# A two-layer decoder trunk on one core: norm blocks in two tiles, sums formed at their source's split, the third block turned early, own tiles for half the output weights

## The chip, the core and the metric

The kernel runs on one core of one Trainium2 chip. The core has a matrix engine (TensorE; PE in the profile, with its weight loads as PEld), a vector engine (DVE), a scalar engine (ACT), a general engine (POOL) and an engine that issues transfers (SP). Each works off its own instructions in order; semaphores tie them together. DMA transfers are issued from SP's, ACT's and POOL's queues; the ones that add to what is already in memory go through POOL's. The metric is the device time in microseconds: 1045.73 us, the median of three runs (1043.29 to 1046.05).

## The reference

512 tokens of width 1024 pass two residual layers, each a token mixer and a gated feed-forward block, with a root-mean-square norm ahead of each and one at the end. Everything is float32.

```
def rmsnorm(x, g):
    y = xf * lax.rsqrt(jnp.mean(xf * xf, axis=-1, keepdims=True) + EPS)
    return (y * g.astype(jnp.float32)).astype(x.dtype)

def swiglu(h, w_gate, w_up, w_down):
    return jnp.einsum('bsf,fd->bsd', jax.nn.silu(g) * u, w_down)    # g, u = h @ w_gate, h @ w_up

for i in range(DEPTH):
    h = rmsnorm(x, norm_mix[i])
    y = pool_mixer(...) if i % N_MIXERS == 0 else attn_mixer(...)
    x = x + y
    h = rmsnorm(x, norm_ffn[i])
    x = x + swiglu(h, w_gate[i], w_up[i], w_down[i])
return rmsnorm(x, norm_final)
```

Layer 0 mixes by windowed means (2, 4, 8 and 16 tokens) with a projection in, a product by group and a projection out; layer 1 by dilated windowed attention with 16 heads, merged by weights over three groups of heads, and a projection out. The feed-forward width is 2816.

## The kernel before

**Products in three parts.** Every float32 operand is split into a rounded part and a rest (`hi`, `lo`): ACT casts (L137 for weights, L302 elsewhere), DVE subtracts (L138, L303). A product is three matmuls, hi x hi, hi x lo and lo x hi.

**Weights.** All weights stand in one list, `queue`, in the order in which they are used. `load` (L93) issues the transfer of an operand into a raw tile of 512 KB (`wraw`, five buffers; `vraw`, three buffers, in the feed-forward blocks alone) from SP. Where an operand is the sum of two blocks of a weight, the second block is added by a transfer on POOL's queue (L105). `weights(i)` (L118) loads up to `load_ahead` operands beyond `i` (or the operand's own `ahead`) and splits up to `split_ahead`, as long as fewer than `RING` = 5 split operands are held; split operands lie in five pairs of tiles of `wspl`.

**Feed-forward.** The products are made by a scheme of Strassen's kind: a group of columns ("quad") has seven operands, 0 to 6. Operands 0 and 3 are plain blocks, 1, 4 and 6 are loaded (1 and 4 as sums of two blocks), and 2 and 5 are formed from operand 1's raw tile by adding operand 0's, then operand 3's raw tile (`plus`, L134). Operands 1, 2 and 5 share one `vraw` tile. The add stands at the split of operand 2 or 5, so the raw tiles of operands 0 and 3 are held until then. `FFN_ORDER` says what follows what: two groups woven together (`TWO`: operands 0 and 3 of both, then 1, 2, 4, 5, 6), two to three single groups, a down projection of the groups so far (`down`, also seven operands), and so on; the last down projection is made plainly, token block by token block (L709). In the woven pair the tokens of blocks 2 and 3 arrive late, in the steps of `late`.

**Norm.** Tokens come in four blocks of 128. `Norm.add` squares half a block on ACT and sums it (L265). `inverse_rms` adds the halves (L273), takes a root on ACT (L274) and refines the inverse in four DVE steps (L275 to L282). `scale` multiplies the block with that and the gain in one DVE instruction (L290) into `xn`, of which there is one. `turn` then transposes `xn` on PE (L299), and `split` writes the tokens, feature by row, into `h` (L302, L303). `h` is written at two offsets, `tokens_at(0)` and `tokens_at(SHIFT)`, so that a new set of tokens can be written beside the old one.

**Around a mixer's end.** `out_projection` (L332) makes the left half of the columns weight by weight for all four blocks, then the right half block by block, and turns block 0 after the products of block 1 and block 1 after those of block 2. Blocks 2 and 3 are turned in the feed-forward block (L622). At the end of the first feed-forward block, blocks 0 and 1 are turned within it (L720), block 2 at the start of attention (`late(2)`, L926) and block 3 between the first products there.

**Order.** PE's instructions keep the order of the text (`manual_schedule`). Those of the other engines, transfers included, are ordered by a planner which goes by program order as priority, by `high_priority`, and by modelled times.

Of the kernel before, what the change touches and what calls it, by code (L numbers as in the profile page):

```python
# [17 lines left out]
P = 128  # L18
S = 512
# [38 lines left out]
def trunk_kernel(ctx: ExitStack, tc: tile.TileContext, x_in, xT, gam, gains, consts, ident_d, w0, wT, w1, wv, w_down, out):  # L58
# [21 lines left out]

    queue = []
# [36 lines left out]
    def weights(i, split_ahead=4, load_ahead=5, held=0):  # L118
# [7 lines left out]
        while len(ready) < min(loaded["w"], i + split_ahead) and (len(ready) <= i or len(ready) - i + held < RING):  # L126
            item = queue[len(ready)]
            if "v" not in pools and item["kind"] == "v":
                break
# [3 lines left out]
            if "plus" in item:  # L133
                nc.vector.tensor_add(raw[:, :n], raw[:, :n], raws[item["plus"]][:, :n])  # L134
            hi = wspl.tile([P, 1024], F32R, name="whi")
            lo = wspl.tile([P, 1024], F32R, name="wlo")
            nc.scalar.copy(hi[:, :n], raw[:, :n])  # L137
            nc.vector.tensor_sub(lo[:, :n], raw[:, :n], hi[:, :n].bitcast(F32))  # L138
# [8 lines left out]
    def rows_of(w):  # L147

        by = w.rearrange("(k p) c -> p k c", p=P)
        return lambda at, half: enqueue(by[:, at : at + 2, COLS[half]], (2, S), rows=True)  # L150
# [8 lines left out]
    j_out += [w_out(BY_GROUP[i], 0) for i in (2, 4, 6)] + [w_out(BY_GROUP[i], 1) for i in (0, 2, 4, 6)]  # L159

    def enqueue_ffn(layer):
# [3 lines left out]
        def operand(js, i, block, shape, ahead):  # L165
# [12 lines left out]
        def quad(n, i, ahead=8):  # L178
# [6 lines left out]
        def down(b):  # L185
# [3 lines left out]
            for i in range(7):  # L189
                for js, a, n in zip(dn[b], (at, at + 2), (2, len(pairs) - 2)):  # L190
                    operand(js, i, lambda m, k: tiles[k, :, a : a + n, COLS[m]], (n, S), 6)
# [20 lines left out]
    j_wo = [wo(2 * i, half) for half in range(2) for i in range(4)]  # L212
# [18 lines left out]
    h_both = [stat.tile([P, NC * S + SHIFT], F32R, name=f"h_{part}") for part in ("hi", "lo")]  # L231

    def tokens_at(shift):
        at = (shift, SHIFT - shift)
        return [h[:, i : i + NC * S].rearrange("p (c s) -> p c s", c=NC) for i, h in zip(at, h_both)]
# [6 lines left out]
    tmp.tile([P, 8], F32, name="gap4")  # L242
    ones = tmp.tile([P, D], F32, name="xn")[:, :P]
# [8 lines left out]
    class Norm:  # L252


        def __init__(self, i=None):
            self.ss = tmp.tile([P, 4, 2], F32, name="ss")
            if i is not None:
                self.gain = tmp.tile([P, D], F32, name="gain")
                nc.sync.dma_start(self.gain, gains[i : i + 1, :].partition_broadcast(P))
                self.xn = tmp.tile([P, D], F32, name="xn")  # L260

        def add(self, b, half):
            sq = tmp.tile([P, S], F32, name="sq")
            with tc.high_priority(URGENT):
                nc.scalar.activation(  # L265
                    sq, x[:, b, COLS[half]], AF.Square, scale=D ** -0.5, accum_out=self.ss[:, b, half : half + 1]
                )

        def inverse_rms(self, b, n=1):

            v, r0, r = (tmp.tile([P, 4], F32, name=name, bufs=2)[:, :n] for name in ("v4", "r04", "r4"))
            sums = self.ss[:, b : b + n, :]
            nc.vector.scalar_tensor_tensor(v, sums[:, :, 0], EPS, sums[:, :, 1], op0=ALU.add, op1=ALU.add)  # L273
            nc.scalar.activation(r0, v, AF.Sqrt)  # L274
            nc.vector.reciprocal(r0, r0)  # L275
            if n == 1:
                nc.vector.tensor_scalar(v, v, r0, r0, op0=ALU.mult, op1=ALU.mult)
            else:
                nc.vector.tensor_mul(v, v, r0)
                nc.vector.tensor_mul(v, v, r0)  # L280
            nc.vector.tensor_scalar(v, v, -0.5, 1.5, op0=ALU.mult, op1=ALU.add)
            nc.vector.tensor_mul(r, v, r0)  # L282
            return r

        def scale(self, b, to, parts):

            with tc.high_priority(URGENT):
# [877 lines left out]
```

## Time and profile before

| what | us |
|---|---|
| median of three runs | 1045.73 |
| the profiled execution | 1047.32 |
| its span | 1045.5 |
| PE busy in the span | 1008.1 |
| DVE busy | 796.5 |
| ACT busy | 510.4 |
| POOL busy | 122.3 |

The span is the time between the profile's first and last event; the 1.8 us between it and the execution's own time lie outside. A busy PE is not a PE at its full rate: where the granted clock falls below 1.00, matmuls start farther apart. A wait is put down to the event that came last before it ended; a row of the timeline gives start, length, engine, line, what is written from what, and in brackets the idle time before it and its releaser. The stages in the profiled execution: the pooling mixer to about 114 us, the first feed-forward block from 114 to 467, attention from 467 to 697, the second feed-forward block from 697 to the end.

### The profile page before, as it was taken

To read this page: it belongs to the slowest core of one execution; us is meant where nothing else is said; L and a number is where in the kernel's file an instruction comes from. 1 tells how busy PE (TensorE), PEld (TensorE's weight loads), DVE (VectorE), ACT (ScalarE), POOL (GpSimd) and SP (SyncE) were. 2 spreads that over 40 slices of the span, in tenths; PEclk is the share of its full clock that TensorE was granted. 3 is DMA by queue.
4 is the path that set the end of the run, shared out by engine and by line. 5 is a ranking of instruction groups with operands and counts; after the bars stand their busy time and mean duration, and the time that the engine had idled before them with its cause. 6 is when DMAs were issued, how large, how long until landed. Compare 5 with 4: busy or idle time off the path is not lost.

```text
span 1045.5 us, 16597 instructions
## 1 busy us (share of the span) xinstructions
PE 1008.1 (96%) x6582; PEld 917.3 (88%) x6582; DVE 796.5 (76%) x1122; ACT 510.4 (49%) x818; POOL 122.3 (12%) x109
## 2 busy tenths in 40 slices
PE   9999978999999999989999999999999999999997
PEld 7888878988998998979778899889898999899895
DVE  5364779897888888776988745479889798788875
ACT  5553355644553654552344443356654465365453
POOL 0000101102011100002324210100110201110000
PEclk9999989999999999999999999999999999999999
DMA  9333557668768855523211242705756965886522
GB/s 350 138 125 77 136 140 181 168 169 220 177 152 221 219 141 150 181 76 112 81 64 40 66 130 93 193 5 164 195 156 188 227 170 123 234 210 160 149 76 80
DMA packets 76349, 155.16 MB, mean 148 GB/s; under 512 B 6448, under 2 KB 6576, under 8 KB 76272
## 3 DMA queue, kind: packets, MB, share of 16 engines
q1 hardware_dynamic: 58800, 120.48, 34.9%
q0 software_dynamic: 17184, 33.36, 18.8%
q8 instruction: 51, 0.84, 0.3%
q10 hardware_dynamic: 288, 0.27, 0.1%
q14 instruction: 26, 0.21, 0.1%
HBM read 151.99 MB, written 2.10 MB: 147 GB/s over the span
## 4 chain that ended last, share of the span: by engine, by line
PE 80%; DMA 8%; DVE 7%; ACT 2%; issue 2%; POOL 0%; SPq 0%; ACTq 0%; POOLq 0%; DVEq 0%
PE p L572 21%; PE r L572 10%; PE r L658 6%; PE mm L572 5%; DMA wraw<-w 5%; PE mm L216 4%; PE mm L217 4%; PE mm L218 4%; PE p L658 3%; DMA vraw<-w 3%; PE mm L709 2%; DVE wlo L138 2%; PE mm L344 2%; PE mm L342 2%; PE mm L343 2%
## 5 line engine op out<-in xcount | busy, mean ns | idle before, releaser
L138 DVE TENSOR_TENSOR wlo<-wraw,whi 128x1024 fp32r<-128x1024 f32 (+2 forms) x198 | 227.9, 1157 | 87.8 <-ACT whi L137 87.4
L137 ACT CAST whi<-wraw 128x1024 fp32r<-128x1024 f32 (+2 forms) x198 | 192.6, 980 | 175.7 <-DMA wraw<-w 32.6
L137 ACT CAST whi<-vraw 128x1024 fp32r<-128x1024 f32 (+1 forms) x102 | 99.4, 975 | 146.1 <-DVE vraw L134 71.3
L572 PE MATMUL p<-t_hi,whi 128*128 128x256 f32 x528 | 151.9, 288 | 12.3 <-ACT keep L583 5.1
L572 PE MATMUL p<-t_hi,wlo 128*128 128x256 f32 x528 | 151.2, 286 | 1.5 <-DVE wlo L138 1.5
L572 PE MATMUL p<-t_lo,whi 128*128 128x256 f32 x528 | 150.8, 286 | 0.0
L138 DVE TENSOR_TENSOR wlo<-vraw,whi 128x1024 fp32r<-128x1024 f32 (+1 forms) x102 | 114.9, 1127 | 33.0 <-ACT whi L137 32.9
L572 PEld LDWEIGHTS p<-t_hi,whi 128*128 128x128 f32 x528 | 101.7, 193 | 14.3 <-ACT keep L583 5.9
L572 PEld LDWEIGHTS p<-t_hi,wlo 128*128 128x128 f32 x528 | 101.7, 193 | 1.9 <-DVE wlo L138 1.9
L572 PE MATMUL r<-h_hi,whi 128*128 128x256 f32 x352 | 99.9, 284 | 2.5 <-ACT h_hi L302 2.5
L572 PEld LDWEIGHTS p<-t_lo,whi 128*128 128x128 f32 x528 | 101.6, 192 | 0.0
L572 PE MATMUL r<-h_lo,whi 128*128 128x256 f32 x352 | 100.1, 284 | 1.0 <-DVE h_lo L303 1.0
L572 PE MATMUL r<-h_hi,wlo 128*128 128x256 f32 x352 | 100.1, 284 | 0.0
L134 DVE TENSOR_TENSOR vraw<-vraw,wraw 128x1024 f32<-128x1024 f32 x68 | 76.6, 1126 | 0.7
L572 PEld LDWEIGHTS r<-h_hi,whi 128*128 128x128 f32 x352 | 67.2, 191 | 2.7 <-ACT h_hi L302 2.7
L572 PEld LDWEIGHTS r<-h_lo,whi 128*128 128x128 f32 x352 | 67.0, 190 | 1.2 <-DVE h_lo L303 1.2
L572 PEld LDWEIGHTS r<-h_hi,wlo 128*128 128x128 f32 x352 | 67.1, 191 | 0.0
L216 PE MATMUL mm<-h_hi,whi 128*128 128x512 f32 (+1 forms) x176 | 66.1, 376 | 0.0
L105 POOL DMA_DIRECT2D wraw<-w x22 | 27.0, 1227 | 330.0 <-DVE x L330 106.4
L217 PE MATMUL mm<-h_lo,whi 128*128 128x512 f32 (+1 forms) x176 | 64.0, 364 | 0.0
L218 PE MATMUL mm<-h_hi,wlo 128*128 128x512 f32 (+1 forms) x176 | 63.9, 363 | 0.0
L105 POOL DMA_DIRECT2D vraw<-w x22 | 26.8, 1227 | 287.9 <-DMA vraw<-w 112.5
(289 smaller groups left out, 2518.1 us busy)
## 6 DMA issues: line engine op xcount, KB each, us to landing
wraw<-w SPq DMA_DIRECT2D x116, 512.0 KB, 4.5
wraw<-w_down SPq DMA_DIRECT2D x32, 512.0 KB, 4.1
wraw<-w POOLq DMA_DIRECT2D x22, 512.0 KB, 9.3
vraw<-w SPq DMA_DIRECT2D x22, 512.0 KB, 5.1
vraw<-w POOLq DMA_DIRECT2D x22, 512.0 KB, 7.2
wraw<-wT SPq DMA_DIRECT2D x16, 512.0 KB, 4.1
wraw<-w_down SPq DMA_DIRECT2D x24, 256.0 KB, 2.7
vraw<-w_down SPq DMA_DIRECT2D x6, 512.0 KB, 5.1
```

Of the source, the lines that this page charges most:

```text
L105: nc.gpsimd.dma_start(dst, more, accum_op=ALU.add)
L134: nc.vector.tensor_add(raw[:, :n], raw[:, :n], raws[item["plus"]][:, :n])
L137: nc.scalar.copy(hi[:, :n], raw[:, :n])
L138: nc.vector.tensor_sub(lo[:, :n], raw[:, :n], hi[:, :n].bitcast(F32))
L216: nc.tensor.matmul(ps, lhsT=whi, rhs=xhi, start=first, stop=False, **kw)
L217: nc.tensor.matmul(ps, lhsT=whi, rhs=xlo, start=False, stop=False, **kw)
L218: nc.tensor.matmul(ps, lhsT=wlo, rhs=xhi, start=False, stop=last, **kw)
L342: nc.tensor.matmul(ps, lhsT=xhi, rhs=w[0][:, k, :], start=first, stop=False)
L343: nc.tensor.matmul(ps, lhsT=xhi, rhs=w[1][:, k, :], start=False, stop=False)
L344: nc.tensor.matmul(ps, lhsT=xlo, rhs=w[0][:, k, :], start=False, stop=last)
L572: nc.tensor.matmul(ps[:, g, :], lhsT=w[:, g, c, :], rhs=xx[:, c, :], start=i in (0, 1, 3) and g + c + k == 0, stop=c == 3 and k == 2, skip ...
L658: nc.tensor.matmul(acc[t], lhsT=u, rhs=w, start=i in (0, 1, 3) and c + k == 0, stop=c == len(pairs) - 1 and k == 2, skip_group_check=True,)
```

## The change

- **Sums.** `plus` is gone. Behind the split of operand 1, operand 0's raw tile is added to operand 1's; behind the split of operand 2 or 3, whichever is later, operand 3's is. Operands 2 and 5 are then split without an add. The look-ahead of groups is 10 instead of 8, that of down projections 10 instead of 6.
- **Ring.** The four weights of the right half of each output projection get their own tiles (pool `b`, four pairs) and don't count in the ring of five; `out_projection` may split and load further ahead.
- **Norm.** A block is multiplied with the gain on DVE, half by half, as soon as it is complete (`gained`); the square's own output goes to the same tile first. Blocks 0 and 2 have one tile, 1 and 3 another (`odd_rows`). The sums are quartered and `EPS / 4` is added to the first of them. The root is taken on ACT directly from the two sums; DVE forms `1 / (v / s + s)`. ACT scales the block.
- **Third block.** `out_projection` transposes block 2 at its own end and hands the result on; the first feed-forward block turns blocks 0, 1 and 2 itself.
- **Memory.** `z` in the pooling mixer and the merged heads of attention are written over `h` at offset 0; `h` is longer by `SHIFT`, and both of its parts use the same offset. One set of window constants is loaded into a tile that the squares use. The angles get their own tile, loaded from SP instead of POOL. In the last stage the output leaves from the norm's tiles instead of `x`.

The core of the diff:

```diff
-        while len(ready) < min(loaded["w"], i + split_ahead) and (len(ready) <= i or len(ready) - i + held < RING):
+        while len(ready) < min(loaded["w"], i + split_ahead):
...
+            if "pool" not in item and len(ready) > i and held + sum("pool" not in it for it in queue[i : len(ready)]) >= RING:
                 break
...
-            if "plus" in item:
-                nc.vector.tensor_add(raw[:, :n], raw[:, :n], raws[item["plus"]][:, :n])
...
             nc.vector.tensor_sub(lo[:, :n], raw[:, :n], hi[:, :n].bitcast(F32))
+            for into, more in item.get("then", ()):
+                nc.vector.tensor_add(raws[into][:, :n], raws[into][:, :n], raws[more][:, :n])
...
-                item.update(into=js[1], plus=js[0 if i == 2 else 3])
+                item.update(into=js[1])
...
+            if i == 1:
+                item["then"] = [(js[1], js[0])]
+            elif i in (2, 3) and 2 in js and 3 in js:
+                item["then"] = [(js[1], js[3])]
...
+        def inverse_rms(self, b):
+
+            v, s, r = (tmp.tile([P, 1], F32, name=name, bufs=2) for name in ("v1", "s1", "r1"))
+            first, second = self.ss[:, b, 0:1], self.ss[:, b, 1:2]
+            nc.scalar.activation(s, second, AF.Sqrt, bias=first)
+            nc.vector.tensor_add(v, first, second)
+            nc.vector.reciprocal(r, s)
+            nc.vector.tensor_scalar(v, v, r, s, op0=ALU.mult, op1=ALU.add)
+            nc.vector.reciprocal(r, v)
             return r
...
+                    nc.scalar.activation(t[:, cs], t[:, cs], AF.Copy, scale=r)
...
-        ws = [weights(js[4 + i], held=i) for i in range(4)]
+        ws = [weights(js[4 + i], split_ahead=4 + i, load_ahead=6 + i) for i in range(4)]
         for b in range(4):
+            norm.gained(b, 0)
...
-            norm.add(b, 1)
+            norm.square(b, 1)
+            norm.gained(b, 1)
             if b < 3:
                 norm.prepare(b)
+        tps = [mm.tile([P, S], F32, name="mm").rearrange("p (j t) -> p j t", j=4) for _ in range(2)]
+        for half in range(2):
+            norm.turn(2, half, tps[half])
+        return tps
...
+            TURNS = {(2, 0): 0, (2, 1): 1, (3, 1): 2}
...
-        late(2)
         norm.prepare(3, COLS)
```

More of the change, by code (lines that the diff above doesn't have):

```diff
@@ L269, in inverse_rms @@
[L269 to L282, printed above, removed]
-            return r
@@ L322, in turned @@
         for half, tp in enumerate(tps):
-            norm.turn(half, tp)
+            norm.turn(b, half, tp)
             (to_hi, src), (to_lo, _) = order(hi, half, tp), order(lo, half, tp)
@@ L405, in trunk_kernel @@
         w_second = [weights(j, held=i) for i, j in enumerate(j_in[1])]
-        norm = Norm()
+        norm = Norm(None, spare)
         for b in range(4):
@@ L410, in trunk_kernel @@
             for half in range(2):
-                norm.add(b, half)
+                norm.square(b, half)
         nc.sync.dma_start(ident, ident_d)
         for k in range(2):
-            bands = tmp.tile([P, D], F32, name=("xn", "gain")[k])[:, : 4 * SPAN].rearrange("p (g j) -> p g j", g=4)
+            bands = (spare, tmp.tile([P, D], F32, name="gain"))[k][:, : 4 * SPAN].rearrange("p (g j) -> p g j", g=4)
             nc.sync.dma_start(bands.rearrange("p g j -> p (g j)"), consts[:, 4 * SPAN * k : 4 * SPAN * (k + 1)])
@@ L418, in trunk_kernel @@
                 nc.vector.tensor_sub(bands_lo, bands[:, :, :HEAD], bands_hi[:, k, :, :HEAD].bitcast(F32))
-        r = norm.inverse_rms(0, 4)
+        v, s, r = (tmp.tile([P, 4], F32, name=name) for name in ("v4", "s4", "r4"))
+        nc.vector.tensor_add(v, norm.ss[:, :, 0], norm.ss[:, :, 1])
+        nc.scalar.activation(s, v, AF.Sqrt)
+        nc.vector.reciprocal(r, s)
+        nc.vector.tensor_mul(v, v, r)
+        nc.vector.tensor_add(v, v, s)
+        nc.vector.reciprocal(r, v)
         def u_out(b, half, ps):
@@ L476, in trunk_kernel @@
         windows(1, range(2, 4))
-        norm = Norm(0)
+        held.close()
+        pools["b"] = open_pool("poolb", 4)
+        px = open_pool("poolx", 1)
+        norm = Norm(0, px.tile([P, D], F32, name="even_rows"))
         banks = [early[0:2], early[2:4]]
@@ L482, in turned_banks, with ffn @@
             return [t.rearrange("p (j t) -> p j t", j=4) for t in banks[-1]]
-        out_projection(j_out, BY_GROUP, z_hi, z_lo, norm, SHIFT, [mm.tile([P, S], F32, name="mm") for _ in range(4)], turned_banks, lambda: group_products(1, early))
-    def ffn(layer, norm, nxt):
+        third = out_projection(j_out, BY_GROUP, z_hi, z_lo, norm, SHIFT, [mm.tile([P, S], F32, name="mm") for _ in range(4)], turned_banks, lambda: group_products(1, early))
+    def ffn(layer, norm, third, nxt):
         gu, dn = j_ffn[layer]
@@ L675, in ffn @@
                             b = 2 + at // 2
-                            late_banks[b] = [r_tile(), by_four(mm.tile([P, S], F32, name="mm"))]
-                            late(b, "turn")
+                            if b == 2:
+                                late_banks[b] = third
+                                norm.prepare(3, COLS)
+                            else:
+                                late_banks[b] = [r_tile(), by_four(mm.tile([P, S], F32, name="mm"))]
+                                for half in range(2):
+                                    norm.turn(b, half, late_banks[b][half])
                             late(b, 1)
-                            if b == 2:
-                                norm.prepare(3, COLS)
                         if at == 4:
@@ L742, in ffn @@
                         close(b, half, ps)
-                        if half == 1 and final:
-                            emit(b)
-            if not final:
-                norm.prepare(0)
+                        if half == 1:
+                            emit(b) if final else norm.prepare(b)
             for b in (2, 3):
@@ L751, in ffn @@
                         products(ps, b, half, z)
-                    if not final and (b, half) in ((2, 1), (3, 0)):
-                        turn_block(b - 2)
+                    if not final and (b, half) in TURNS:
+                        turn_block(TURNS[b, half])
                     close(b, half, ps)
@@ L768, in trunk_kernel @@
         ptr = actx.enter_context(tc.tile_pool(name="ptr", bufs=2, space=bass.MemoryType.PSUM))
+        at = 8 * SPAN
+        angles = aw.tile([P, D], F32, name="angles", bufs=1)
+        cosr, sinr = (angles[:, cs] for cs in COLS)
+        nc.sync.dma_start(angles, consts[:, at : at + D])
         pT = ap.tile([P, 6 * 7 + 10 * 4, P], F32, name="pT")
@@ L1094, in trunk_kernel @@
         four = [t.rearrange("p r j -> p (r j)") for t in four]
-        out_projection(j_wo, range(NC), m_hi, m_lo, norm, SHIFT, four, lambda: [sc_tile(), sc_tile()])
-    ffn(1, norm, 3)
+        third = out_projection(j_wo, range(NC), m_hi, m_lo, norm, SHIFT, four, lambda: [sc_tile(), sc_tile()])
+    ffn(1, norm, third, 3)
 def _constants():
```

114 lines of the change are left out of this document (57 added, 57 removed).

## The prediction

> **What bounds the kernel now.** I read the busy shares first, then the waits of PE, then the stretches in which those waits lie, then the neighbours of each wait on ACT, SP and POOL.
>
> ```profile
> PE 1008.1 (96%) x6582; PEld 917.3 (88%) x6582; DVE 796.5 (76%) x1122; ACT 510.4 (49%) x818; POOL 122.3 (12%) x109
> ```
>
> PE is the bound, and the change removes none of its matmuls. So only time in which PE stands still, or runs slowly, can be won. PE's waits, grouped:
>
> ```profile
> PE p L572 <- ACT keep L583: 5.1, 4, 2.0
> PE tp L299 <- DVE r L275: 5.1, 1, 5.1
> PE p L572 <- ACT ct L587: 3.9, 1, 3.9
> PE p L572 <- ACT whi L137: 3.2, 2, 1.6
> PE r L299 <- DVE xn L290: 2.9, 2, 1.7
> PE r L572 <- ACT h_hi L302: 2.5, 1, 2.5
> PE p L572 <- DVE wlo L138: 1.5, 2, 0.8
> ```
>
> The columns are total us, times and the longest. They lie in few places. The stretches below give length, busy time of PE, PEld, DVE, ACT and POOL, then granted clock, DMA share and GB/s:
>
> ```profile
> 28.00:43.00 15.00, 14.70 (x83) 12.62 (x81) 7.78 (x17) 13.03 (x29) 0.00 (x0) 1.00 0.50 187
> 114.40:182.60 68.20, 56.81 (x427) 55.19 (x427) 54.49 (x73) 33.82 (x50) 8.48 (x7) 0.92 0.69 173
> 242.70:305.00 62.30, 60.33 (x505) 59.96 (x504) 49.43 (x57) 33.55 (x44) 6.98 (x6) 1.00 0.74 184
> 443.40:472.20 28.80, 23.75 (x114) 19.48 (x113) 21.16 (x42) 16.14 (x33) 0.00 (x0) 0.99 0.27 86
> 472.20:490.00 17.80, 17.80 (x139) 17.80 (x140) 7.45 (x13) 3.55 (x6) 2.44 (x3) 0.92 0.28 88
> 697.00:755.50 58.50, 54.39 (x427) 53.55 (x427) 54.52 (x73) 33.72 (x49) 4.82 (x4) 0.94 0.57 149
> ```
>
> Loss in a stretch is PE's idle time plus length times (1 - clock), since a stall is also paid for in slow matmuls behind it. The opening of the first FFN, 114.4 to 182.6: 68.2 - 56.8 = 11.4 idle and 0.08 x 68.2 = 5.5 slow, **16.9 us**. The opening of the second, 697.0 to 755.5: 4.1 and 3.5, **7.6 us**. The turn into attention, the two rows around 472: 5.05 idle and 1.4 slow, **6.4 us**. The four waits for `keep`, **5.1 us**; one is the 1.97 us idle of 242.7 to 305.0, just behind a down projection. Together 36 us.
>
> Why the openings stall shows on the queues. SP, POOL and ACT, each in time order:
>
> ```profile
> 114.34 1.39 SPq L103 DMA_DIRECT2D vraw<-w  x3
> 122.93 0.34 SPq L259 DMA_DIRECT2D gain<-gains  x1
> 134.32 17.61 SPq L103 DMA_DIRECT2D wraw<-w  x5
> ```
> ```profile
> 118.55 1.21 POOL L105 DMA_DIRECT2D vraw<-w  x1 [25.11 <-PE p L572]
> 120.15 2.57 POOL L105 DMA_DIRECT2D vraw<-w  x2 [0.40 <-DMA vraw<-w]
> 138.43 1.21 POOL L105 DMA_DIRECT2D wraw<-w  x1 [15.71 <-ACT ct L585]
> ```
> ```profile
> 148.10 1.04 ACT L137 CAST whi<-wraw 128x1024 fp32r<-128x1024 f32 x1 [5.62 <-DMA wraw<-w]
> 149.05 0.58 ACT L302 CAST h_hi<-mm 128x512 fp32r<-128x512 f32 x1
> 149.53 0.59 ACT L587 COPY ct<-p 128x512 f32<-128x512 f32 x1
> ```
>
> No plain weight load is issued between 114 and 134.32: the five raw buffers hold operands 0 and 3 of both groups, kept for sums that the old code forms only at operands 2 and 5. The load that gets the first freed buffer needs an accumulate at 138.43, which lands near 148.0. ACT's cast waits for it 5.62 us, and behind it stands the copy of `p` (L587) for which PE waits 3.9 us. A late DMA thus stops PE by way of ACT's order.
>
> **The change part by part.**
>
> *Sums at their source's split.* The adds stay as many; each moves one to three operands earlier, behind the subtraction of the split before it. Removed is an add ahead of a cast:
>
> ```profile
> L137 ACT CAST whi<-vraw 128x1024 fp32r<-128x1024 f32 (+1 forms) x102 | 99.4, 975 | 146.1 <-DVE vraw L134 71.3
> ```
>
> ACT waited 71.3 us in all for the add. Mostly this is hidden under PE; it shows in the waits for `whi` and `wlo` (3.2 + 1.5 us), once in each opening. The raw buffer of operand 3 comes free at the split of operand 2 instead of 5, three products earlier, that of operand 0 one earlier. The loads behind them move forward by as much, with their POOL accumulates; the look-ahead (8 and 6 becoming 10) lets SP use it. This bears on the first opening and on the waits for `keep`.
>
> *The first opening* (16.9 us). The wait for `xn` (half of 2.9) should go by the norm's change. The waits for `h_hi` and `ct` and the slow matmuls behind them hang on sums that land late. The `v` loads are issued at 114.34, when the projection's last matmul ends, and I assume no more than some 2 us for that: the output weights' own tiles lie where those buffers will be, and the last of them is read until the end as well. The later accumulate gains more: its slot comes free when operand 1 is split. That operand's accumulate is issued at 118.55; if it lands as fast as the one of 138.43 (9.6 us), cast, subtraction and add (1.0 + 1.2 + 1.2) are over at 131.6, some 3 us before 134.32, and earlier if it lands faster. DVE sets a floor: 54.5 us busy, of which some 3 us (two splits of 1.2 us, a gain product) can run ahead in the projection, so 51.5, and at most 68.2 - 51.5 = 16.7 can be won with a DVE that never waits. I take **12**; bounds 4 (only `xn` and `whi`) and 16.7.
>
> *The second opening* (7.6 us). The same floor: 54.5 - 3 = 51.5 against 58.5, at most 7.0. I take **5**, bounds 1 and 7.
>
> *Own tiles for half the output weights.* Eight weights in all leave the ring of five; no instruction is added. It lets the first four feed-forward operands be split in the projection; counted above.
>
> *The norm.* The small steps are read at the kernel's end, DVE and then ACT:
>
> ```profile
> 1039.13 0.69 DVE L717 TENSOR_TENSOR xn<-x,gain 128x512 f32<-128x512 f32 x1
> 1039.94 0.16 DVE L273 SCALAR_TENSOR_TENSOR v<-ss 128x1 f32<-128x1 f32 x1
> 1040.37 0.16 DVE L275 RECIPROCAL r<-r 128x1 f32<-128x1 f32 x1 [0.27 <-ACT r L274]
> 1040.57 0.27 DVE L277 TENSOR_SCALAR v<-v,r 128x1 f32<-128x1 f32 x1
> 1040.88 0.15 DVE L281 TENSOR_SCALAR v<-v 128x1 f32<-128x1 f32 x1
> 1041.07 0.16 DVE L282 TENSOR_TENSOR r<-v,r 128x1 f32<-128x1 f32 x1
> ```
> ```profile
> 1040.14 0.20 ACT L274 ACTIVATE r<-v 128x1 f32<-128x1 f32 x1 [0.23 <-DVE v L273]
> 1041.32 0.72 ACT L732 ACTIVATE x<-xn,r 128x512 f32<-128x512 f32 x1 [0.98 <-DVE r L282]
> ```
>
> Root before: add, hop to ACT, root, hop back, four DVE steps. After: the root follows the square on ACT at once, then reciprocal, one fused step, reciprocal. Off the chain go L273 with its hop (1039.94 to 1040.14, 0.2 us) and one step of 0.19 us: **0.4 us a block**. A block's product with `r` and gain was one DVE instruction:
>
> ```profile
> 469.64 1.22 DVE L138 TENSOR_TENSOR wlo<-wraw,whi 128x1024 fp32r<-128x1024 f32 x1
> 470.78 1.28 DVE L290 SCALAR_TENSOR_TENSOR xn<-x,r,gain 128x1024 f32<-128x1024 f32 x1
> ```
>
> It becomes two gain products of 0.69 on DVE, ahead of the root, and a scaling on ACT. That 1024-wide scaling is not in the trace; it lies between 1.04 (the cast above) and 2 x 0.72 = 1.44, I take 1.2, so the chain keeps its last step. DVE sheds 1.28 + 3 x 0.16 and takes 1.38 + 3 x 0.16 a block: no change. ACT takes 1.2 more a block, 19 us over sixteen blocks; it is 34 of 68 us busy in the opening and 16 of 29 at 443.4, so idle time covers it, unless it stands behind a waiting cast (a rival). On this place the Trainium skill speaks against the change: "ScalarE: Activation LUTs", section "Rules for kernel authors", puts multiplications on VectorE. By it the twelve hidden scalings would be a loss; the sum goes by the rows, 1.28 against 1.2.
>
> *Two tiles and the third block early.* With one `xn`, a block's product had to wait for the turn of the block before it. At 470.78 block 2 was scaled only behind weight splits (the row above it ends 0.1 us before), and PE waited 5.1 us at its turn. Now block 2 is scaled under the two products of block 3, 24 matmuls or 5.4 us at 0.227 us apiece (the 72 of L709 in this stretch take 16.4), against a chain of adding (0.69), squaring (0.6 + 0.2), root (0.2 + 0.8) and scaling (1.2), 3.7 us before queueing. Its turn then needs no wait; what is late next is block 3, whose turn has 48 matmuls of 0.12 us = 5.7 us of cover. I take **5.5** of 6.4, bounds 2 and 6.4.
>
> *Behind the down projections* (5.1 us for `keep`): a raw buffer freed one product (2.9 us, 24 matmuls) to three earlier against a wait of at most 2.0. I take **4**, bounds 0 and 5.1.
>
> *The end.* 0.4 us from the root, and the last addition no longer stands behind a DVE scaling (0.7 at most); the last gain product now waits for its square, which wrote the same tile (-0.4): **0.7**, bounds -1 and 1.1. Outputs now leave from the norm's tiles, so the square of block 2 waits for the transfer of block 0; block 3's 24 matmuls (5.4 us) lie between.
>
> *What is added.* In 28 to 43 the window constants are loaded into a tile that two squares use first, so their SP issue moves from 24 to 33 and what SP holds behind it too:
>
> ```profile
> xn<-consts SPq DMA_DIRECT2D x1, 288.0 KB, 7.5
> ```
>
> The windows begin at 38.4, so a landing of 7.5 us is 2 to 3 us late and one of 4 us is in time, now that nothing else loads: **-1**, bounds -3 and 0. The angles move from POOL's queue to SP's and wait there for feed-forward memory; behind them stand loads that are needed ten us later: 0, bounds -1 and 0. `z` and the merged heads now lie on `h`. Were the shifted writes held back until the last read, two blocks' splits (0.6 + 0.69, four times) would add up to 5 us at each projection's end; PE reads the pairs of blocks before they are overwritten, so 0. For the rest **-1**.
>
> **Sum.** 12 + 5 + 5.5 + 4 + 0.7 - 1 - 1 = 25.2 us. The profiled execution took 1047.3 us (span 1045.5), 1.6 above the median of the three runs; 1047.3 - 25.2 = 1022.1, from the median 1020.5. I say **1021.5**. By that execution all lower bounds together give 1046, all upper ones 1012.
>
> How far slow matmuls follow what remains is read here:
>
> ```profile
> 176.98 0.39 PE L572 MATMUL p<-t_hi,whi 128*128 128x256 f32 x1 [1.62 <-ACT whi L137]
> ...
> 179.26 0.41 PE L572 MATMUL p<-t_hi,whi 128*128 128x256 f32 x1
> 179.48 0.41 PE L572 MATMUL p<-t_lo,whi 128*128 128x256 f32 x1
> ```
>
> After 1.6 and 0.8 us of idling matmuls start 0.22 us apart instead of 0.12. The Trainium skill, "TensorE: Matmul & The Clock Gate", section "HAM oscillation", asks for idle gaps over about 3.4 us before the clock falls. By that rule the leftover stalls would leave no slow matmuls and I would say some 3 us less; this row does not agree, and I leave about half of the leftover as slow time.
>
> **The rivals.**
>
> *DVE binds the openings.* For it: 54.5 of 58.5 us in the second one. Adds done early are put into DVE's densest stretch, and fewer of its waits can go. Then 5 and 1 remain of 12 and 5, and 3 of 4: 25.2 - 12 = 13, **1034**. Chance 0.22.
>
> *Scalings held behind waiting casts.* For it: 5.6 us at 148.10. Three late blocks (one in each opening, one at attention), each up to 5.6 us: 17 us back, **1039**. Against it: freed buffers make those casts wait less. 0.06.
>
> *Nearly all stalls go*: **1010**. 0.08.
>
> *The planner undoes it.* Vector and scalar orders come from a planner, which may put the adds where they stood, and the loads wait for the same buffers; attention's gain is eaten by the constants: **1045**. 0.06.
>
> *Slower: SP's queue jams.* With a look-ahead of ten, a load waiting for a raw buffer stands before a sum's load whose buffer is free, and copy and accumulate start late in each of the 18 single groups. At the 2.0 us of the longest wait for `keep`, 36 us against 25: **1057**; it decides from 1.4 us a group. Against it: only four of the 18 wait now, DMA is 0.74 busy. 0.08.
>
> **Chances.** Forecast, 1013 to 1031: 0.50. Only differences above 0.3%, 3 us, can be told from none. Faster: 0.50 + 0.22 + 0.06 + 0.08 = 0.86; same 0.06; slower 0.08. The range, 1009 to 1040, leaves out the last two and a little.
>
> **What would show it.** Right: no wait of PE for `r` or `xn` near 472, clock above 0.96 in both openings, ACT's wait for the add nearly gone, a plain load issued before 130. Wrong: DVE without a gap while PE waits for `wlo` (first rival), a scaling on ACT started late behind a cast (second), SP loads later against their product than now (jam).

## The result and the profile after

The changed kernel takes 1019.5 us (median of four runs, 1018.4 to 1021.56); the kernel before, run beside it, 1045.89 (1043.29 to 1052.77). The ratio is 0.974, 95% interval 0.9691 to 0.9789. The forecast was 1021.5 us, range 1009 to 1040. The size is right, and several of its reasons are not: that took the experiments.

The profiled execution of the changed kernel took 1018.4 us, its span is 1016.6. First the busy shares, then PE's waits (total us, times, longest):

```profile
PE 1000.0 (98%) x6582; PEld 912.5 (90%) x6582; DVE 792.8 (78%) x1134; ACT 530.0 (52%) x836; POOL 121.0 (12%) x108
```
```profile
PE r L601 <- ACT h_hi L312: 3.9, 1, 3.9
...
PE p L601 <- ACT ct L616: 0.9, 1, 0.9
PE tp L920 <- ACT pT L925: 0.9, 1, 0.9
PE mm L309 <- ACT even_rows L303: 0.7, 1, 0.7
PE sc L851 <- DVE e L859: 0.6, 1, 0.6
```

The waits for `keep` (5.1 us), for the third block's turn (`r`, 5.1), for `xn` (2.9) and, in the feed-forward blocks, for `whi` and `wlo` are gone. One long wait is left, in the first opening. ACT carries 19.6 us more, as forecast (19), DVE 3.7 less.

To place the gain I cut each trace at the same PE instructions: the first, the 505th (after 21 products of 24 matmuls) and the last matmul of the groups of each feed-forward block. The 21 products are the woven pair and the first single group; this is "the opening" below, and a little longer than the prediction's stretch. Stretches of before, then of after, in the columns of the prediction's windows (length, busy PE, PEld, DVE, ACT, POOL, granted clock, DMA share, GB/s):

```profile
115.17:193.92 78.75, 67.36 (x516) 65.74 (x514) 62.78 (x83) 40.76 (x58) 10.60 (x9) 0.93 0.73 181
697.86:766.71 68.85, 64.74 (x515) 63.90 (x514) 62.64 (x83) 40.00 (x58) 6.93 (x6) 0.95 0.62 162
```
```profile
115.46:185.00 69.54, 64.59 (x515) 63.74 (x514) 58.85 (x77) 41.39 (x58) 10.59 (x9) 0.95 0.79 205
679.46:740.46 61.00, 61.00 (x516) 61.00 (x515) 59.55 (x79) 41.63 (x59) 5.72 (x5) 1.00 0.64 169
```

The second opening has become all PE at full clock. The first has not: 5 us of PE's time are idle, and the clock is 0.95. The whole span, all kernels, by these cuts (us; each from one profiled execution; the last 22.1 us of PE are the same in all but e10's 22.7):

| kernel | to first product | first opening | rest of first block's groups | to second block | second opening | rest of its groups |
|---|---|---|---|---|---|---|
| before | 115.2 | 78.8 | 249.3 | 254.6 | 68.9 | 248.9 |
| changed | 115.5 | 69.5 | 247.0 | 247.5 | 61.0 | 246.9 |
| e1 late sums again | 117.4 | 70.0 | 248.2 | 247.5 | 60.9 | 247.8 |
| e2 early sums alone | 115.3 | 73.3 | 246.7 | 255.6 | 64.9 | 246.7 |
| e3 no own tiles | 115.6 | 73.2 | 246.9 | 248.6 | 63.0 | 246.7 |
| e4 third block late | 115.5 | 69.6 | 247.0 | 247.0 | 60.8 | 246.7 |
| e5 V buffers first | 115.5 | 60.8 | 246.7 | 247.5 | 60.8 | 246.7 |
| e6 norm's part alone | 115.7 | 68.4 | 249.5 | 248.6 | 60.8 | 251.7 |
| e7 one tile | 118.6 | 67.6 | 247.0 | 260.2 | 60.8 | 246.7 |
| e8 scaling on DVE | 116.7 | 72.7 | 246.7 | 247.4 | 60.8 | 246.7 |
| e9 third early alone | 117.7 | 75.4 | 255.3 | 250.3 | 67.8 | 249.8 |
| e10 all but the norm | 118.7 | 72.7 | 248.5 | 255.8 | 61.9 | 248.5 |
| e11 more DVE work | 115.5 | 67.6 | 246.7 | 247.5 | 62.5 | 246.7 |
| e12 look-ahead 8 and 6 | 115.4 | 69.2 | 246.7 | 247.5 | 60.8 | 246.7 |

Before to changed: -0.3 in the first column, then 9.2, 2.4, 7.1, 7.9, 2.0 won, and 0.7 at the end, together 29.0 us; the spans differ by 28.9. PE's busy time falls from 1008.1 to 1000.0 us with the same 6582 matmuls, so 8.1 of the 28.9 are matmuls that now start at the full rate; in the other 20.8 PE no longer stands still. PE's order is the old one but for the turn into attention: the third block's transposes stand just ahead of a block's first product in both kernels (in the first block at 114.38 and at 114.61).

What is left in the first opening is read from PE's long wait backwards. The rows are of the changed kernel: PE, ACT, POOL, SP.

```profile
131.89 0.58 PE L601 MATMUL r<-h_hi,whi 128*128 128x256 f32 x1 [3.86 <-ACT h_hi L312]
```
```profile
127.23 1.05 ACT L137 CAST whi<-vraw 128x1024 fp32r<-128x1024 f32 x1 [6.20 <-DMA vraw<-w]
...
129.76 1.05 ACT L137 CAST whi<-vraw 128x1024 fp32r<-128x1024 f32 x1 [0.99 <-DMA vraw<-w]
131.23 0.61 ACT L312 CAST h_hi<-t1r 128x512 fp32r<-128x512 f32 x1
```
```profile
118.04 1.21 POOL L106 DMA_DIRECT2D vraw<-w  x1 [39.71 <-DMA vraw<-w]
...
122.80 1.23 POOL L106 DMA_DIRECT2D vraw<-w  x1 [1.50 <-DMA vraw<-w]
```
```profile
113.97 1.39 SPq L104 DMA_DIRECT2D vraw<-w  x3
116.62 0.34 SPq L267 DMA_DIRECT2D gain<-gains  x1
131.34 0.37 SPq L104 DMA_DIRECT2D wraw<-w  x1
```

PE waits for a cast of tokens. That cast stands on ACT behind two casts of V, which wait for accumulated loads; their accumulates go out 4 to 9 us after the plain V loads, and those are issued at 113.97, when the output projection has ended. It is the prediction's own mechanism, a late DMA that stops PE by way of ACT's order, with another DMA in it.

### The profile page after: what moved, and what is told of

Same layout as the page of the kernel before. It is cut to its first block, busy times and chain, and to the rows that moved or that the text cites. A ratio compares the mean times of both kernels' runs of the same rounds, so it can differ in the third digit from the quotient of the medians.

```text
span 1016.6 us, 16615 instructions
## 1 busy us (share of the span) xinstructions
PE 1000.0 (98%) x6582; PEld 912.5 (90%) x6582; DVE 792.8 (78%) x1134; ACT 530.0 (52%) x836; POOL 121.0 (12%) x108
## 4 chain that ended last, share of the span: by engine, by line
PE 92%; DVE 3%; DMA 2%; ACT 2%; issue 1%; POOL 0%; SPq 0%; ACTq 0%; POOLq 0%
PE p L601 24%; PE r L601 13%; PE r L684 10%; PE mm L601 6%; PE p L684 5%; PE mm L222 4%; PE mm L224 3%; PE mm L223 3%; PE mm L738 3%; PE mm L684 2%; PE mm L354 2%; PE mm L352 2%; PE mm L353 2%; DMA vraw<-w 1%; PE mm L1073 1%; PE mm L1072 1%
## 5 line engine op out<-in xcount | busy, mean ns | idle before, releaser
L138 DVE TENSOR_TENSOR wlo<-wraw,whi 128x1024 fp32r<-128x1024 f32 (+2 forms) x190 | 220.4, 1161 | 76.6 <-ACT whi L137 76.0
L137 ACT CAST whi<-wraw 128x1024 fp32r<-128x1024 f32 (+2 forms) x190 | 185.2, 978 | 173.0 <-issue 34.7
L137 ACT CAST whi<-vraw 128x1024 fp32r<-128x1024 f32 (+1 forms) x102 | 99.4, 976 | 148.0 <-DVE vraw L140 51.6
L601 PE MATMUL p<-t_hi,whi 128*128 128x256 f32 x528 | 148.7, 282 | 0.9 <-ACT ct L616 0.9
L601 PEld LDWEIGHTS p<-t_lo,whi 128*128 128x128 f32 x528 | 99.3, 188 | 0.1
L601 PEld LDWEIGHTS r<-h_hi,wlo 128*128 128x128 f32 x352 | 67.6, 192 | 0.0
L684 PE MATMUL r<-wlo,u_hi 128*128 128x512 f32 x144 | 56.1, 390 | 0.0
```

Of the source, the lines that this page charges most:

```text
L601: nc.tensor.matmul(ps[:, g, :], lhsT=w[:, g, c, :], rhs=xx[:, c, :], start=i in (0, 1, 3) and g + c + k == 0, stop=c == 3 and k == 2, skip ...
L684: nc.tensor.matmul(acc[t], lhsT=u, rhs=w, start=i in (0, 1, 3) and c + k == 0, stop=c == len(pairs) - 1 and k == 2, skip_group_check=True,)
```

## The experiments

Each was run beside the kernel before on the same chip; ratios are to that.

**e1: the sums put back.**

```diff
+            if "plus" in item:
+                nc.vector.tensor_add(raw[:, :n], raw[:, :n], raws[item["plus"]][:, :n])
...
-            for into, more in item.get("then", ()):
-                nc.vector.tensor_add(raws[into][:, :n], raws[into][:, :n], raws[more][:, :n])
...
-                item.update(into=js[1])
+                item.update(into=js[1], plus=js[0 if i == 2 else 3])
```

> The changed kernel (1019.5 us, its ratio 0.974), with operands 2 and 5 summed again at their own split; look-ahead of ten, own tiles, norm and third block stay changed. Theory (the early sums free the raw buffers, and that removed the stalls in both feed-forward openings and behind the down projections, some 8.6 + 8 + 6 us): most of these come back, 1032 to 1040 us, with a wait of PE for keep and a late plain weight load in the openings. Rival (look-ahead of ten and own tiles removed them; the place of the add is hidden anyway): 1018 to 1023 us.

Measured: 1023.66 us, ratio 0.9817 (0.977 to 0.9863). The span is 4.5 us longer than the changed kernel's, and 2.0 of that lie in the first 10 us, where nothing was edited: there the matmuls start 0.43 us apart until 9.8 us, in the changed kernel only until 6.3 and then 0.23 apart. (The same holds of the profiled executions of e7, e8 and e9 and adds 1.9, 1.6 and 2.4 us to their first column.) The openings are unmoved (70.0 and 60.9 against 69.5 and 61.0). Only the waits behind the down projections are back:

```profile
PE p L597 <- ACT keep L608: 3.2, 3, 1.7
```

So the theory on the openings fell: in the finished kernel they don't depend on where the sums stand. For the first opening this is shown only with its other stall in place; that stall goes in e5, and there the sums were not put back.

**e2: the early sums alone**, in the kernel before (the same lines the other way).

> The kernel before (1045.9 us) with the sums alone formed at their source's split; look-ahead 8 and 6, ring of five, one xn, third block late. Theory: 10 to 18 us faster, 1028 to 1036 us; the wait for r near 472 stays. Rival (without the longer look-ahead SP doesn't use the freed buffers): 0 to 4 us faster, 1042 to 1046 us.

Measured: 1037.23 us, ratio 0.9924 (0.9893 to 0.9956): 7 us by the medians, less than the theory's 10 to 18, more than the rival's. No wait for `keep` is left (246.7 twice, with the old look-ahead). The profiled execution is the fastest of the six, 1034.32 us, and its span is 13.0 us shorter, not 7. In it the openings give 5.5 and 4.0 us; only 2.7 and 1.0 of these are waits. The rest is mostly matmuls at the full rate, which an execution can have or not (last section). The turn into attention stays as it was, as foreseen.

**e3: all output weights in the ring again.**

```diff
-[w_out(BY_GROUP[i], 1, pool="b") for i in (0, 2, 4, 6)]
+[w_out(BY_GROUP[i], 1) for i in (0, 2, 4, 6)]
...
-        ws = [weights(js[4 + i], split_ahead=4 + i, load_ahead=6 + i) for i in range(4)]
+        ws = [weights(js[4 + i], held=i) for i in range(4)]
...
-        pools["b"] = open_pool("poolb", 4)
```

> The changed kernel with all eight output weights in the ring of five again and without the pool of own tiles; the rest stays. Theory (own tiles only let a few splits run ahead of the openings): 1 to 5 us back, 1020 to 1025 us, lost in the first 20 us of the two openings. Rival (own tiles carry the openings' gain): 8 to 17 us back, 1028 to 1037 us. Second rival (their memory lies under the three V buffers and holds the V loads until the projection's end, so without them the first opening gets better): 2 to 6 us faster than changed, 1013 to 1018 us.

Measured: 1025.5 us, ratio 0.9818 (0.9781 to 0.9854). The openings lose 3.6 and 2.0 us: just past the upper end of the theory, far from the first rival. Of the 3.6, PE's waits make 1.1 (6.0 against 4.9 us idle); the rest is slow matmuls. The second rival's gain didn't show: without own tiles the V loads still go out only at 115.96, when the third block's turn has ended, and later in the first opening a cast on ACT waits 5.5 us for a plain load.

**e4: the third block turned late**, at the start of attention.

```diff
-            TURNS = {(2, 0): 0, (2, 1): 1, (3, 1): 2}
+            TURNS = {(2, 1): 0, (3, 0): 1}
...
+        late(2)
         norm.prepare(3, COLS)
```

> The changed kernel with the third block turned at the start of attention as before, after the first and second at their old places; two tiles and the new chain stay. Theory (the turn's place hides the chain): 3 to 5 us back, 1022 to 1025 us, with a wait of PE for the third block's turn near 470. Rival (two tiles and the shorter chain suffice): within 1 us of the changed kernel.

Here the third block's tile lies in memory that attention has taken over when it is turned, so its tokens there aren't the reference's; the instructions and their waits are the same. Measured: 1017.46 us, ratio 0.9744 (0.9703 to 0.9785), no slower than the changed kernel. The rival holds: with two tiles and the new chain the third block's turn waits 0.5 us at the old place and not at all at the new one.

**e5: the V buffers' memory moved.** The three V buffers of the first block lay under the output weights' own tiles; opened first, they lie under the group products' operands, which are read for the last time at 73.7 us, 40 us earlier.

```diff
+            pools["v"] = open_pool("ffv", V_TILES)
             fp = open_pool("ffn", 1)
             fps = open_pool("ffps", 2, space=bass.MemoryType.PSUM)
-            pools["v"] = open_pool("ffv", V_TILES)
```

> The changed kernel with the pool of the three V buffers opened first in the feed-forward block, so that in the first block it lies under the group products' operands (last read near 90 us) and no longer under the output weights' own tiles (last read near 114). Theory (the stall of 4.0 + 3.0 us at 128 to 137, and the 1.3 behind it, hang on V loads that are issued only at 113.97): the V loads go out before 105, that stall goes, 4 to 8 us faster than the changed kernel (1018 to 1020), 1011 to 1016 us. Rival (DVE and ACT are full there and the waits only change their names): within 2 us of the changed kernel.

Measured: **1010.01 us** (1008.89 to 1011.25), ratio 0.9657 (0.962 to 0.9695): faster than both kernels. SP, POOL, then the first opening:

```profile
74.11 1.39 SPq L104 DMA_DIRECT2D vraw<-w  x3
```
```profile
79.92 1.21 POOL L106 DMA_DIRECT2D vraw<-w  x1 [1.52 <-PE mm L354]
81.33 1.20 POOL L106 DMA_DIRECT2D vraw<-w  x1 [0.21 <-issue]
85.14 1.23 POOL L106 DMA_DIRECT2D vraw<-w  x1 [2.60 <-issue]
```
```profile
115.49:176.25 60.76, 60.76 (x515) 60.76 (x514) 57.49 (x76) 41.00 (x57) 5.75 (x5) 1.00 0.63 170
```

The V loads go out 40 us earlier. The opening is as short as the second one, 60.8 us of PE at full clock. So the 113.97 was worth 69.5 - 60.8 = 8.8 us: the stall and the slow matmuls behind it, and the 0.9 for `ct` too. Whether the same move alone would mend the first opening of the kernel before, whose V loads go out at 114.34, was not tried.

**e6: the norm's part alone**: e1 and e3 together, with the look-ahead of 8 and 6.

> The changed kernel without the early sums, without own tiles and with the look-ahead of 8 and 6: what is left is the norm in two tiles, its chain, the third block early and the memory. If early sums and own tiles each suffice for the openings (putting back one cost 0 and 6 us there): the openings now lose most of what they lost before, together some 17 to 24 of 26 us, keep waits 4 to 6 us return, and the turn into attention stays mended: 1032 to 1039 us. If the norm's part carries the openings: 1024 to 1029 us.

Measured: 1025.93 us, ratio 0.9807 (0.9752 to 0.9862), the second answer. Its openings:

```profile
115.69:184.11 68.42, 64.42 (x516) 63.61 (x514) 58.44 (x78) 40.14 (x58) 10.59 (x9) 0.95 0.79 204
682.13:742.90 60.77, 60.77 (x516) 60.77 (x513) 59.12 (x79) 40.73 (x59) 6.93 (x6) 1.00 0.68 180
```

Both are as short as with everything, with late sums and the old ring. The waits for `keep` are all there, 6.5 us with slow matmuls behind the last. DVE's work in an opening is some 4 us less than before (58.4 and 59.1 against 62.8 and 62.6), mainly as the scaling of block 3 has gone to ACT (0.8), an addition of the tokens' halves (1.2) and one weight split (1.2) have moved ahead of the first product, and another split (1.2) has moved behind the twenty-first.

**e7: one tile for all blocks.**

```diff
-            self.tiles = [even, odd_rows]
+            self.tiles = [odd_rows, odd_rows]
```

> The changed kernel with one tile for all blocks of the norm; third block early and the new chain stay. Theory (a second tile lets a block be squared and multiplied while the one before is turned): the wait at the third block's turn returns at three places (two projections' ends, the turn into attention), 2 to 5 us each, and the last stage waits for its outputs: 1026 to 1036 us. Rival (the turn's place and the shorter chain do it): within 3 us of the changed kernel.

In this kernel half of a block's product is overwritten by the next block's before it is turned. Measured: 1038.06 us, ratio 0.993 (0.9901 to 0.9959), 2 us past the theory. The turns wait:

```profile
PE r L309 <- ACT odd_rows L303: 3.9, 1, 3.9
PE mm L309 <- DVE odd_rows L284: 3.8, 3, 2.1
PE r L309 <- DVE ss L280: 2.6, 1, 2.6
```

The way to the second block, with the turn into attention and the second projection in it, takes 12.7 us more than in the changed kernel, and 8.6 are lost at the end, where each block now waits for the output of the one before (15.8 us from PE's last matmul to the span's end, 7.1 in the changed kernel). The openings themselves keep their length. As the blocks' order isn't the old kernel's, this shows what sharing costs the new order, not what the second tile won over the old.

**e8: the block scaled on DVE in place of ACT.**

```diff
-                    nc.scalar.activation(t[:, cs], t[:, cs], AF.Copy, scale=r)
+                    nc.vector.tensor_scalar_mul(t[:, cs], t[:, cs], r)
```

> The changed kernel with the block scaled by the inverse root on DVE in place of ACT. By the rows ACT takes 1.15 us for 1024 columns and DVE 0.49 for 512 at the kernel's end, so some 0.9. Theory (DVE is the denser engine in the openings, 54 of 68 us, ACT has room): 0 to 3 us slower than the changed kernel. Rival (the scaling stands behind ACT's waiting casts, and a hop to ACT is saved): 1 to 3 us faster.

Measured: 1021.37 us, ratio 0.9765 (0.9719 to 0.9812), which overlaps the changed kernel's. The instruction itself is shorter, here in e8 and then in the changed kernel:

```profile
115.04 0.75 DVE L303 TENSOR_SCALAR even_rows<-even_rows,r 128x1024 f32<-128x1024 f32 x1
```
```profile
L303 ACT ACTIVATE even_rows<-even_rows,r 128x1024 f32<-128x1024 f32 x4 | 4.6, 1152 | 6.7 <-DVE r L294 6.7
```

The Trainium skill, "ScalarE: Activation LUTs", section "Rules for kernel authors", puts multiplications on VectorE; by the instruction's length it is right here, 0.75 against 1.15 us. The total shows no gain from it. The second opening is as short as with ACT (60.8). In this execution the first is 3.1 us longer (72.7 against 69.5), but not because DVE is full: it is busy 60.4 of the 72.7 us. Its order is another one. The split of the tokens there stands behind a weight's split and an addition, and PE waits for it, which it doesn't in the changed kernel:

```profile
131.84 1.22 DVE L138 TENSOR_TENSOR wlo<-vraw,whi 128x1024 fp32r<-128x1024 f32 x1 [0.95 <-ACT whi L137]
132.98 1.22 DVE L140 TENSOR_TENSOR vraw<-vraw,wraw 128x1024 f32<-128x1024 f32 x1
134.12 0.68 DVE L313 TENSOR_TENSOR h_lo<-t1r,h_hi 128x512 fp32r<-128x512 f32 x1
```
```profile
134.86 0.58 PE L601 MATMUL r<-h_lo,whi 128*128 128x256 f32 x1 [2.00 <-DVE h_lo L313]
```

So neither the theory (DVE is the denser engine) nor the rival is shown.

**e9: the third block early, alone**, in the kernel before: turned at the projections' end and at the first block's end, one `xn`, old chain.

```diff
+        tps = [mm.tile([P, S], F32, name="mm").rearrange("p (j t) -> p j t", j=4) for _ in range(2)]
+        for half in range(2):
+            norm.turn(half, tps[half])
+        return tps
...
-                    if not final and (b, half) in ((2, 1), (3, 0)):
+                    if not final and (b, half) in TURNS:
```

> The kernel before with the third block alone turned early, at the projections' end and in the first feed-forward block; one xn, the old chain, one DVE instruction a block, late sums. The norm's part without it, e6, is 20 us faster than before. Theory (a product moved ahead of the opening takes its DVE work with it, so the place does most): the openings from first to twenty-first product, 78.8 and 68.9 us before, fall to 70 to 74 and 62 to 65, but the turn itself now waits at the projections' end, 2 to 4 us each, and 2 to 4 us at attention: 1032 to 1039 us in all. Rival (two tiles do it: with one xn the turn waits for a chain of some 4 us, and the rest of the openings stays): 1042 to 1048 us.

Measured: 1039.75 us, ratio 0.9934 (0.9908 to 0.9961). The median's 7 us can't be placed: the profiled execution, 1047.95 us, is the slowest of the ten and no shorter than the one of the kernel before. Its waits can be compared. In the openings PE stands still for 11.2 and 4.1 us, as before (11.4 and 4.1), and the 3.4 and 1.0 us that they are shorter are nearly all matmuls at full rate. The way to the second block falls by 4.3. At attention, 5.1 us of waiting become 1.5. So for that turn either remedy does: two tiles and the new chain (e4), or the place (this one). For the openings the place does nothing that these waits show, and PE's order there is the old one anyway.

**e10: all of the change but the norm**: e2 with the look-ahead, the own tiles and the memory. A filler tile of 32 bytes was left out to make room.

> All of the change but the norm: early sums, look-ahead of ten, own tiles, the heads and z over h; old norm with one xn, third block late. By the prediction's steps (12 us in the first opening, 5 in the second, 4 behind the down projections from these parts, less 1 to 2 for the waits for xn): 1025 to 1030 us. If the norm carries the openings, as e6 has it: the openings stay within 3 us of the sums alone (73.3 and 64.9 us), 1033 to 1039 us.

Measured: 1038.16 us, ratio 0.9926 (0.9903 to 0.9949). The openings:

```profile
118.71:191.41 72.70, 64.39 (x516) 63.51 (x514) 60.45 (x80) 41.05 (x58) 10.60 (x9) 0.95 0.78 199
695.67:757.61 61.94, 61.54 (x516) 61.10 (x514) 60.58 (x81) 40.43 (x57) 5.73 (x5) 1.00 0.62 166
```

Time and openings are those of the second answer, the second opening only just (61.9 against 64.9). Against the kernel before, though, 6.1 and 6.9 us are won there. The total hides this, because the kernel loses elsewhere: 3.5 us ahead of the first product and 0.8 in each of six down projections (below).

**e11: 3.7 us more work for DVE in the second opening.**

```diff
-                            first_tokens(1, b21r)
+                            for _ in range(1 + 3 * layer):
+                                first_tokens(1, b21r)
```

> The changed kernel with three more DVE additions of 1.22 us (first_tokens again, the same values) in the second opening alone. There DVE is 59.6 us busy of 61.0 and PE never waits. Theory (DVE is the second bound of the opening, and the 3.5 us of its work that the norm's change moves ahead are what freed PE): 3.7 us are more than the 1.4 left, the second opening grows from 61.0 to 63 to 65 us with waits of PE for splits, 1021 to 1024 us. Rival (the openings were held by loads or by order, not by DVE's load): within 1 us of the changed kernel.

Measured: 1018.65 us, ratio 0.9742 (0.9712 to 0.9773). The second opening, and the wait that came with it:

```profile
677.31:739.85 62.54, 61.32 (x515) 60.93 (x514) 61.93 (x81) 41.73 (x59) 5.72 (x5) 1.00 0.59 159
```
```profile
PE p L601 <- DVE t_lo L313: 1.2, 2, 1.0
```

It grew by 1.5 us, not by the 2 to 4 of the theory; in the total nothing is seen. DVE does come to its limit (61.9 of 62.5 busy), but 3.7 us of work cost 1.5. The 3.1 to 3.5 us of DVE's work by which this opening is lighter than before (62.6 against 59.6, and 59.1 in e6) can then hardly be worth the 7.9 won. Before, this opening lost 4.1 us by waits (1.7 for `xn`, 1.6 for `whi`, 0.8 for `wlo`) and 3.4 by slow matmuls. Which of the norm's edits removes them isn't shown: with one tile (e7) or the scaling on DVE (e8) the opening stays at 60.8, and the third block's place alone (e9) leaves the waits as they were.

**e12: the look-ahead of 8 and 6 again.**

```diff
-        def quad(n, i, ahead=10):
+        def quad(n, i, ahead=8):
...
-COLS[m]], (n, S), 10)
+COLS[m]], (n, S), 6)
```

> The changed kernel with the look-ahead of 8 and 6 again. Theory (the early sums alone free the buffers that the waits for keep hung on, as with the sums alone): no wait for keep, within 1 us of the changed kernel. Rival (SP needs the longer look-ahead to use them): keep waits of 2 to 5 us return, 1021 to 1025 us.

Measured: 1018.3 us, ratio 0.9737 (0.971 to 0.9764), no wait for `keep`. The longer look-ahead does nothing once the sums are early.

## Why the prediction was right, and where it was not

| term | forecast | measured |
|---|---|---|
| first opening | 12 | 9.2 |
| second opening | 5 | 7.9 |
| turn into attention | 5.5 | 7.1 to the second block: 5.4 at the turn, 1.7 inside attention |
| behind the down projections | 4 | 4.4 |
| the end | 0.7 | 0.7 |
| constants and the rest | -2 | -0.3 |
| sum | 25.2 | 29.0 in the profiled pair, 26.4 by the medians |

*First opening.* The step that failed is to hang this stall on the later accumulate, the one of 138.43. The working on it came true: the plain load behind it went from 134.32 to 131.34, where I had 131.6. So did the sentence on the V loads, "I assume no more than some 2 us for that": they went from 114.34 to 113.97. But those loads come first in the same queue and bound the opening: 9.2 us were won of the 12, and e5 wins 8.8 more by nothing but issuing them earlier. The prediction saw the row and the memory under it, and went past them.

*Both openings: whose gain.* I credited the sums and the own tiles and gave the norm a half of 2.9 us. The runs show two halves of the change that do the same work: the norm's part alone wins 10.3 and 8.1 us (e6), all the rest alone 6.1 and 6.9 (e10), both together 9.2 and 7.9. PE's waits alone, without the slow matmuls, say the same: of 11.4 and 4.1 us before, the norm's part alone leaves 4.0 and 0, all the rest alone 8.3 and 0.4, both together 4.9 and 0. In the finished kernel the sums carry nothing there (e1), the own tiles 3.6 and 2.0 (e3). The second opening ended at its floor of 61.0 us, PE at full clock, either way; my bound of 7 came from DVE's work and was too tight, because I let only 3 us of it leave the stretch. From the projection's end to the same matmul as in the prediction's row, 8.0 us are won (58.3 to 50.3), and DVE's work in it falls by 4.7 (54.3 to 49.6).

*Turn into attention.* Right place, right size. That the third block's place was needed is wrong: two tiles with the new chain suffice (e4), and the place alone does most of it too (e9). The 1.7 us inside attention were not foreseen. There PE waits for `e` (L828) 1.5 us before and 0.6 after, and in the profile of before slow matmuls follow, from 536.5 to 539.9, which cost 1.7; in the changed kernel a wait of 0.9 for `pT` is new. Which edit brings this was not tried.

*Down projections.* Right: the early sums win these by themselves (e2), and with late sums they come back (e1, e6). The look-ahead, named as the means, is none (e12).

*The rivals.* SP's queue did not jam; e12 has nothing to win back. The planner did not undo the adds. "DVE binds the openings" had 5 and 1 us where 9.2 and 7.9 came; but e11 does find DVE at its limit in the second one. "Nearly all stalls go" (1010) is not this change, but it is e5, by one more edit. Scalings behind waiting casts: the block scaled on ACT stops PE for 0.7 us in the projection, no more.

*What would show it.* No wait above 0.3 us at the turn into attention, and the second opening at clock 1.00: as said. The first opening at 0.95 and the first plain load at 131.34 (I wanted 130, though my own working gave 131.6) were misses; the first pointed at the V loads. ACT's wait for the add was to be nearly gone; the row of the changed kernel has it at 51.6 us of the 71.3, off PE's path:

```profile
L137 ACT CAST whi<-vraw 128x1024 fp32r<-128x1024 f32 (+1 forms) x102 | 99.4, 976 | 148.0 <-DVE vraw L140 51.6
```

## What to carry to other kernels

Where a stage opens with a stall, look first at when its earliest loads are issued and whose memory they wait for: a pool opened in another order was worth a third as much again as the whole change, with no instruction altered. When several edits aim at one stall, put each back alone and also run each alone; here the early sums, which cost the openings nothing to remove, were still worth some us there by themselves, because another edit had covered them. And compare stage by stage: e10's total would have hidden 13 us won in the openings. But a stage is read from one execution: see that its time is near the median, and compare PE's waits before lengths.

## What the runs showed of the hardware

The same stall is followed by slow matmuls in one execution and not in another. Before, second opening, and then e9 at the same place:

```profile
749.83 0.39 PE L572 MATMUL p<-t_hi,whi 128*128 128x256 f32 x1 [1.62 <-ACT whi L137]
...
751.09 0.39 PE L572 MATMUL p<-t_hi,wlo 128*128 128x256 f32 x1 [0.76 <-DVE wlo L138]
...
751.80 0.42 PE L572 MATMUL p<-t_hi,whi 128*128 128x256 f32 x1
752.02 0.42 PE L572 MATMUL p<-t_lo,whi 128*128 128x256 f32 x1
```
```profile
751.09 0.39 PE L576 MATMUL p<-t_hi,whi 128*128 128x256 f32 x1 [1.62 <-ACT whi L137]
...
752.35 0.39 PE L576 MATMUL p<-t_hi,wlo 128*128 128x256 f32 x1 [0.76 <-DVE wlo L138]
...
752.92 0.28 PE L576 MATMUL p<-t_hi,whi 128*128 128x256 f32 x1
753.03 0.29 PE L576 MATMUL p<-t_lo,whi 128*128 128x256 f32 x1
```

Both idle 1.62 and 0.76 us; then matmuls start 0.22 us apart in the first and 0.12 in the second, where the clock stayed up. The clock records of the traces show why. The granted clock is full or half, and it changes only in steps of 3.41 us that run through the whole execution: in the kernel before it falls at 133.7, 150.8, 178.1, 471.6, 536.5, 707.1 and 751.5 us, whole numbers of steps apart, and each time for one step, which costs 1.7 us. Two steps of the kernel before around this stall, then two of e9:

```profile
748.12:751.53 3.41, 1.02 (x6) 0.74 (x6) 2.30 (x3) 3.29 (x4) 0.00 (x0) 1.00 0.47 138
751.53:754.94 3.41, 3.41 (x18) 3.41 (x17) 2.92 (x3) 0.15 (x1) 0.00 (x0) 0.50 0.23 44
```
```profile
748.04:751.45 3.41, 1.79 (x14) 1.51 (x13) 2.22 (x3) 1.95 (x3) 0.00 (x0) 1.00 0.14 31
751.45:754.86 3.41, 2.65 (x23) 2.52 (x22) 3.41 (x4) 1.48 (x2) 0.00 (x0) 1.00 0.34 130
```

Before, both gaps lie in one step, 2.39 us of idling together, and the next step has half the clock. In e9 the border of the steps lies between them, 1.62 and 0.76, and the clock stays up. In all fourteen profiles a step at full clock with over 2 us of idling was followed by one at half clock, 22 times; with under 1.4 us this happened once (0.3 us, in e10); in between, both occur. Where the borders lie changes from execution to execution (the first rise comes between 4.0 and 10.7 us). That may be why a kernel with such stalls scatters: 1040.06 to 1051.98 us in 17 runs of the kernel before, against 1008.89 to 1011.25 in six of e5, which has none. The Trainium skill, "TensorE: Matmul & The Clock Gate", section "HAM oscillation", gives idle gaps over about 3.4 us as what brings the clock down; the first of the two traces has it after less, and the second fits.

In e10 the matmuls of the down projections start 0.233 us apart in place of 0.227, with no wait and at clock 1.00. The first and the last of the 126 matmuls of the first down projection, in e10 and then in the changed kernel:

```profile
211.43 0.40 PE L665 MATMUL r<-whi,u_hi 128*128 128x512 f32 x1
...
240.60 0.39 PE L665 MATMUL r<-whi,u_lo 128*128 128x512 f32 x1
```
```profile
205.16 0.39 PE L684 MATMUL r<-whi,u_hi 128*128 128x512 f32 x1
...
233.54 0.39 PE L684 MATMUL r<-whi,u_lo 128*128 128x512 f32 x1
```

That is 29.17 against 28.38 us, the 0.8 us named above, and it is the same in all six. The instructions are the same. That it comes from where the tiles lie, and from the missing 32 bytes, is a guess that was not tried.
